# Token norms on all partitions, a table for the reciprocal root, and the order around four norm boundaries

## Chip, core and metric

One NeuronCore of a Trainium2 chip (trn2) runs the whole program. TensorE (PE) multiplies matrices, VectorE (DVE) and ScalarE (ACT) work elementwise, GpSimd (POOL) does little here, and SyncE (SP) issues most of the DMAs. The metric is the device time of one execution in microseconds (us), lower is better.

## The reference

A two-layer decoder trunk for one sequence of 256 tokens, D = 2048. Each layer has a token mixer (gated linear attention, GLA, in layer 0; forgetting attention, FoX, in layer 1) and a gated MLP with a short convolution (FFN). Each of the four sub-layers starts with the same norm, and a fifth stands at the end:

```
def rmsnorm(x, gain):
    xf = xf * lax.rsqrt(jnp.mean(xf * xf, axis=-1, keepdims=True) + NORM_EPS)
    return xf * gain

for i in range(2):
    mod = silu(c) @ w_mod[i] + b_mod[i]          # six vectors: shift, scale, gate, twice
    h = rmsnorm(x, norm_mix[i]) * (1.0 + sc_m) + sh_m
    x = x + (1.0 + g_m) * mixer(h)               # GLA, then FoX
    h = rmsnorm(x, norm_ffn[i]) * (1.0 + sc_f) + sh_f
    x = x + (1.0 + g_f) * conv_ffn(h, ...)
return rmsnorm(x, norm_final)
```

## The kernel before

**Layout.** The residual x stays in SBUF as `xT`: features on the 128 partitions, 16 slices m of 128 features, each 128x256 (256 tokens). A token's norm is therefore a sum over partitions and over slices.

**Products.** Every large product streams its weights from HBM in tiles k of 128x1024 float32 (SP issues the loads, five slots). A tile is split in two halves of a shorter format: ACT casts the high part (`wh`, L114), DVE subtracts (`wl`, L115). The activations are split in the same way (`h` high by ACT, L465; `h` low by DVE, L466 and L467), and PE adds three matmuls for each block: high times high (L544), low h times high w (L545), high h times low w (L546). `wh` and `wl` have four buffers each (AHEAD + 1), so the cast of tile k has to wait until PE is done with tile k-4. The last three tiles (TAIL) of a product that ends a sub-layer are held back and finished bank by bank, and DVE adds each bank to `xT` (L600).

**The norm.** While the tail runs, ACT squares the new slices two at a time (`sq`, L398, 128x512), DVE adds the early ones into `ss` (L404), and PE sums `ss` and the last two `sq` over partitions by matmuls against a vector of ones (L411: two columns of `pm`, tokens on partitions). `token_rstd` (L420 to L433) makes the reciprocal root of two columns on DVE: a bit shift as a first guess and three Newton steps, 15 small instructions. `bcast_cols` turns the two columns back into a row on all partitions: two diagonal matrices on DVE (`dg`, L367) and two matmuls (L369). `make_h` then makes the operand slice by slice: `hn` = xT times that row (L464), high part with scale and shift (L465), low part (L466, L467).

**Order.** A list scheduler sets the order of each engine's instructions when the kernel is built; `tc.issue_after` pins single instructions behind others. Engines run their queues strictly in that order. `gate` pins the casts of the four tiles that follow slice m=1 behind the last square and behind the low part of m=1.

**Side work.** The six modulation vectors of the next sub-layer are made beside the main work: weights by DMA, products and sums on DVE into `acc` (L250, L252, 128x1024), then `finish` reduces `acc` over partitions by PE transposes (L265) and ACT activations with an accumulated sum (L274). Ahead of FoX and of the second FFN two such finishes are deferred into the wait at the norm.

**The boundaries.** The prediction calls them A (start, into GLA), B (GLA into the first FFN), C (first FFN into FoX), D (FoX into the second FFN) and E (end: final norm, eight blocks of the output scaled by DVE and ACT, L1228 to L1233, and eight output DMAs, all on SP, L1234). FoX starts with a narrow product (L591 to L593) and has wide matmuls of 512 columns (L577 to L579).

## Time and profile before

| | |
|---|---|
| time, median of 3 runs | 2486.22 us (2484.94 to 2488.49) |
| the profiled execution | 2486.61 us, its span 2484.9 us |
| PE busy | 2421.4 us, 97% of the span |
| DVE busy | 1906.7 us, 77% |
| ACT busy | 1279.8 us, 52% |
| mean granted TensorE clock | 0.984 |

The span runs from the first instruction to the last on the profiler's clock; 1.7 us of the profiled execution lie around it. Times within the span are counted from its start. The granted clock is 1.00 at 2.4 GHz and 0.50 at 1.2 GHz.

### The profile page before, as it was taken

To read this page: it belongs to the slowest core of one execution; us is meant where nothing else is said; L and a number is where in the kernel's file an instruction comes from. 1 tells how busy PE (TensorE), PEld (TensorE's weight loads), DVE (VectorE), ACT (ScalarE), POOL (GpSimd) and SP (SyncE) were. 2 spreads that over 40 slices of the span, in tenths; PEclk is the share of its full clock that TensorE was granted. 3 is DMA by queue.
4 is the path that set the end of the run, shared out by engine and by line. 5 is a ranking of instruction groups with operands and counts; after the bars stand their busy time and mean duration, and the time that the engine had idled before them with its cause. 6 is when DMAs were issued, how large, how long until landed. Compare 5 with 4: busy or idle time off the path is not lost.

```text
span 2484.9 us, 47584 instructions
## 1 busy us (share of the span) xinstructions
PE 2421.4 (97%) x19242; PEld 2331.1 (94%) x19242; DVE 1906.7 (77%) x2570; ACT 1279.8 (52%) x1956; POOL 14.6 (1%) x35
## 2 busy tenths in 40 slices
PE   6999999899999999999999999999999999999998
PEld 6988899899999999999988888999999999999998
DVE  6776989886789999977587888887776777767544
ACT  2446554444655666543454555554655556565433
POOL 0000000000000000000000000000000000000000
PEclk7999999999999999999999999999999999999999
DMA  8897878798668998899589887687677777766553
GB/s 349 268 309 239 295 262 287 269 317 306 207 195 270 309 308 301 285 314 316 179 278 308 304 280 235 212 293 268 197 236 232 231 235 232 233 193 218 192 192 122
DMA packets 184314, 638.36 MB, mean 257 GB/s; under 512 B 23962, under 2 KB 24972, under 8 KB 183709
## 3 DMA queue, kind: packets, MB, share of 16 engines
q1 hardware_dynamic: 183704, 635.17, 77.1%
q8 instruction: 150, 2.46, 0.4%
q14 instruction: 72, 0.58, 0.1%
q10 hardware_dynamic: 388, 0.15, 0.0%
HBM read 633.14 MB, written 2.10 MB: 256 GB/s over the span
## 4 chain that ended last, share of the span: by engine, by line
PE 74%; DMA 11%; DVE 9%; issue 3%; ACT 2%; SPq 0%; DVEq 0%; ACTq 0%
PE pa L545 19%; PE pa L546 19%; PE pa L544 19%; DMA wm<-in_w_mod_dram 6%; PE pa L579 4%; PE pa L578 4%; PE pa L577 4%; DVE wl L115 4%; DVE acc L252 2%; DMA w<-in_ffn_w_down_dram 2%; DMA w<-in_ffn_w_up_dram 2%; ACT wh L114 1%; DMA w<-in_gla_w_out_dram 1%; PE pm L265 1%; PE pm L411 0%
## 5 line engine op out<-in xcount | busy, mean ns | idle before, releaser
L114 ACT CAST wh<-w 128x1024 fp32r<-128x1024 f32 x819 | 856.4, 1048 | 1033.7 <-PE pa L545 463.7
L115 DVE TENSOR_TENSOR wl<-w,wh 128x1024 fp32r<-128x1024 f32 x819 | 994.8, 1218 | 365.0 <-ACT wh L114 354.2
L544 PE MATMUL pa<-h,wh 128*128 128x256 f32 x3584 | 990.1, 278 | 10.1 <-ACT h L465 5.6
L545 PE MATMUL pa<-h,wh 128*128 128x256 f32 x3584 | 993.1, 278 | 1.1 <-DVE h L467 0.9
L546 PE MATMUL pa<-h,wl 128*128 128x256 f32 x3584 | 991.7, 278 | 1.5 <-DVE wl L115 1.5
L544 PEld LDWEIGHTS pa<-h,wh 128*128 128x128 f32 x3584 | 674.2, 189 | 12.0 <-ACT h L465 6.6
L546 PEld LDWEIGHTS pa<-h,wl 128*128 128x128 f32 x3584 | 675.0, 189 | 4.4 <-issue 2.3
L545 PEld LDWEIGHTS pa<-h,wh 128*128 128x128 f32 x3584 | 676.9, 189 | 2.0 <-DVE h L467 1.7
L252 DVE SCALAR_TENSOR_TENSOR acc<-wm,cT,acc 128x1024 f32<-128x1024 f32 x352 | 450.7, 1280 | 125.2 <-DMA wm<-in_w_mod_dram 123.5
L544 PE MATMUL pa<-op,wh 128*128 128x256 f32 x1920 | 527.2, 277 | 5.2 <-DVE xT L600 2.9
L545 PE MATMUL pa<-op,wh 128*128 128x256 f32 x1920 | 526.8, 277 | 2.0 <-DVE op L483 2.0
L546 PE MATMUL pa<-op,wl 128*128 128x256 f32 x1920 | 518.4, 278 | 1.6 <-DVE wl L115 1.0
L544 PEld LDWEIGHTS pa<-op,wh 128*128 128x128 f32 x1920 | 360.8, 188 | 6.6 <-DVE xT L600 3.4
L545 PEld LDWEIGHTS pa<-op,wh 128*128 128x128 f32 x1920 | 361.3, 188 | 2.2 <-DVE op L483 2.2
L546 PEld LDWEIGHTS pa<-op,wl 128*128 128x128 f32 x1920 | 354.9, 188 | 4.3 <-DVE wl L115 4.0
L578 PE MATMUL pa<-wh,h 128*128 128x512 f32 x512 | 200.4, 392 | 0.0
L577 PE MATMUL pa<-wh,h 128*128 128x512 f32 x512 | 199.2, 392 | 0.6 <-ACT wh L114 0.6
L579 PE MATMUL pa<-wl,h 128*128 128x512 f32 x512 | 193.9, 395 | 0.6 <-DVE wl L115 0.5
L577 PEld LDWEIGHTS pa<-wh,h 128*128 128x128 f32 x512 | 96.4, 188 | 20.7 <-ACT wh L114 1.0
L579 PEld LDWEIGHTS pa<-wl,h 128*128 128x128 f32 x512 | 95.9, 188 | 20.8 <-DVE wl L115 2.0
L578 PEld LDWEIGHTS pa<-wh,h 128*128 128x128 f32 x512 | 96.2, 188 | 19.8 <-issue 0.2
L1043 ACT ACTIVATE y<-u,cw 128x256 f32<-128x256 f32 x176 | 101.8, 600 | 17.1 <-DVE act L1059 14.7
(236 smaller groups left out, 1392.7 us busy)
## 6 DMA issues: line engine op xcount, KB each, us to landing
wm<-in_w_mod_dram SPq DMA_DIRECT2D x352, 512.0 KB, 5.2
w<-in_ffn_w_up_dram SPq DMA_DIRECT2D x320, 512.0 KB, 4.5
w<-in_ffn_w_down_dram SPq DMA_DIRECT2D x176, 512.0 KB, 4.6
w<-in_fox_w_in_dram SPq DMA_DIRECT2D x128, 512.0 KB, 5.2
...
```

What stands on the lines that cost most here:

```text
L114: nc.scalar.copy(out=hi, in_=src)
L115: order["v"] = nc.vector.tensor_tensor(out=lo, in0=src, in1=hi.bitcast(F32), op=ALU.subtract).ins
L252: nc.vector.scalar_tensor_tensor(out=st["a"], in0=wt[:, j, :], scalar=col, in1=st["a"], op0=ALU.mult, op1=ALU.add)
L265: nc.tensor.transpose(pt[:, m * P:(m + 1) * P], st["a"][:, (q0 + m) * P:(q0 + m + 1) * P], ident)
L544: nc.tensor.matmul(o, wh[:, ms], rh, start=(first and m % 2 == 0), stop=False, skip_group_check=True)
L545: nc.tensor.matmul(o, wh[:, ms], rl, start=False, stop=False, skip_group_check=True)
L546: nc.tensor.matmul(o, wl[:, ms], rh, start=False, stop=last, skip_group_check=True)
L577: nc.tensor.matmul(o, lh[:, ts_], wh[:, hs_], start=first, stop=False)
L578: nc.tensor.matmul(o, ll[:, ts_], wh[:, hs_], start=False, stop=False)
L579: nc.tensor.matmul(o, lh[:, ts_], wl[:, hs_], start=False, stop=last)
L1043: nc.scalar.activation(y, u, AF.Identity, scale=cw[:, l * 3 + 2, r:r + 1], bias=cw[:, 6 + l, r:r + 1])
```

## The change

Six things change.

1. The sum over partitions uses a held matrix `onesD` (all entries 1/D) as one operand, so that the mean lands on all partitions at once as 128x256. `half_sum` first adds the two halves of `ss` on DVE, and the last square is split in two of 128x256. The final norm (`fin`) keeps two columns.
2. `token_rstd` takes a table function of ACT (`Abs_reciprocal_sqrt`) and one third-order step of five DVE instructions, on 128x256 (on 128x2 at E). The broadcast (`dg`, L369, the copy of `rb`) goes. A small activation `warm` behind the square of m=12 brings the table load forward.
3. Deferred finishes (C and D) reduce by eight matmuls against a column of ones instead of transposes and ACT sums; one of the two runs ahead of the tail.
4. `split_to` is called ahead of the tail, and the gate now holds three casts instead of four, behind the high part (`hot`) and the low part of m=1. The `hn` of m=1 to 3 are pinned behind the low part of the slice ahead.
5. The helper for other reciprocal roots (GLA and FoX, off the boundaries) loses two DVE instructions per call.
6. At E four of the eight output DMAs are issued by ACT.

```diff
-        for j in range(2):
-            for tt in range(TT):
-                order["s"] = nc.tensor.matmul(ss["p"][:, tt:tt + 1], sq[:, j, tt * P:(tt + 1) * P], one, ...)
+        if not fin:
+            order["s"] = nc.tensor.matmul(ss["p"][:, :T], onesD, sq, start=first, stop=last, skip_group_check=True).ins
+            return
...
+        if end and m == KT - 2:
+            for j in range(2):
+                order["a"] = nc.scalar.activation(sq[:, j, :], xT[:, m + j, :], AF.Square).ins
+                token_sum(sq[:, j, :], False, j == 1)
+            return
...
             if m == KT - NTS:
-                token_sum(ss["t"], True, False)
-            token_sum(sq, False, m == KT - 2)
+                warm = tmp.tile([P, 1], F32, tag="warm", bufs=1, name=nm("warm"))
+                nc.scalar.activation(warm, sq[:, 0, 0:1], AF.Abs_reciprocal_sqrt, bias=epsc)
+                half_sum()
+                token_sum(ss["t"][:, 0, :], True, False)
+            for j in range(2):
+                token_sum(sq[:, j, :], False, False)
...
+    def token_rstd(q, n_):
+        nc.scalar.activation(q, ss["p"][:, :n_], AF.Abs_reciprocal_sqrt, bias=epsc)
+        ...
+        nc.vector.scalar_tensor_tensor(out=t, in0=ss["p"][:, :n_], scalar=EPS, in1=q, op0=ALU.add, op1=ALU.mult)
+        nc.vector.tensor_tensor(out=t, in0=t, in1=q, op=ALU.mult)
+        nc.vector.tensor_scalar(out=p, in0=t, scalar1=0.375, scalar2=-1.25, op0=ALU.mult, op1=ALU.add)
+        nc.vector.tensor_tensor(out=t, in0=t, in1=p, op=ALU.mult)
+        nc.vector.scalar_tensor_tensor(out=q, in0=t, scalar=1.875, in1=q, op0=ALU.add, op1=ALU.mult)
...
-        pb = bcast_cols([rs[:, 0:1], rs[:, 1:2]], -1.0)
-            if m == 2:
-                nc.scalar.copy(out=rb, in_=pb[:, :T])
-            nc.vector.tensor_tensor(out=t, in0=xT[:, m, :], in1=pb[:, :T] if m < 2 else rb, op=ALU.mult)
-            nc.scalar.activation(hi, t, AF.Identity, scale=sc, bias=sh)
+            with ExitStack() as es:
+                if 0 < m < 4:
+                    es.enter_context(tc.issue_after(st["lo"]))
+                nc.vector.tensor_tensor(out=t, in0=xT[:, m, :], in1=rb, op=ALU.mult)
+            hot = nc.scalar.activation(hi, t, AF.Identity, scale=sc, bias=sh).ins
             ...
             ins = nc.vector.tensor_tensor(out=lo, in0=t, in1=hi.bitcast(F32), op=ALU.subtract).ins
+            st["lo"] = ins
             if m == 1:
-                gate["n"], gate["ins"] = AHEAD + 1, [order["a"], ins]
+                gate["n"], gate["ins"] = AHEAD, [hot, ins]
...
         if done is not None:
+            split_to(min(fetched["use"] + 1, len(plan)))
+            if deferred:
+                deferred.pop(0)()
...
+                if defer:
+                    pt = psA.tile([P, 512], F32, tag="a", name=nm("pt"))
+                    for m in range(mn):
+                        nc.tensor.matmul(pt[:, m:m + 1], st["a"][:, m * P:(m + 1) * P], one, start=(m == 0), ...)
...
-            nc.sync.dma_start(out=out[0, tt * P:(tt + 1) * P, cs], in_=dst)
+            (nc.sync if tt == 0 else nc.scalar).dma_start(out=out[0, tt * P:(tt + 1) * P, cs], in_=dst)
```

What this does to the queues is seen at two boundaries. DVE at B, from the low part of slice 1 on; `hn` and `h` are the slices of the operand (m counted from 0), `wl` the low halves of the weight tiles k=1 to 4 of the first FFN. Before:

```order
L467 TENSOR_TENSOR h_5040<-hn_5046,h_5040 128x256
L115 TENSOR_TENSOR wl_5060<-w_4831,wh_5059 128x1024
L115 TENSOR_TENSOR wl_5066<-w_4861,wh_5065 128x1024
L115 TENSOR_TENSOR wl_5072<-w_4891,wh_5071 128x1024
L466 TENSOR_SCALAR hn_5052<-hn_5052,mod 128x256
L464 TENSOR_TENSOR hn_5191<-xT,rb_5029 128x256
L466 TENSOR_SCALAR hn_5103<-hn_5103,mod 128x256
L466 TENSOR_SCALAR hn_5147<-hn_5147,mod 128x256
L467 TENSOR_TENSOR h_5040<-hn_5052,h_5040 128x256
L115 TENSOR_TENSOR wl_5111<-w_5057,wh_5110 128x1024
L467 TENSOR_TENSOR h_5040<-hn_5103,h_5040 128x256
```

The last row is the low part of slice 3; the row above it is tile k=4. And now, DVE at B from the low part of slice 2 on (first row) to that of slice 3 (last row); `wl_5114` is tile k=5, `wl_5158` tile k=6:

```order
L487 TENSOR_TENSOR h_5000<-hn_5011,h_5000 128x256
L484 TENSOR_TENSOR hn_5062<-xT,rb_4981 128x256
L484 TENSOR_TENSOR hn_5106<-xT,rb_4981 128x256
L484 TENSOR_TENSOR hn_5150<-xT,rb_4981 128x256
L115 TENSOR_TENSOR wl_5114<-w_5022,wh_5113 128x1024
L199 COPY cw<-pm_5144 128x352
L254 TENSOR_SCALAR acc_5097<-wm_5058,cT 128x1024
...
L486 TENSOR_SCALAR hn_5062<-hn_5062,mod 128x256
...
L256 SCALAR_TENSOR_TENSOR acc_5097<-wm_5060,cT,acc_5097 128x1024
L115 TENSOR_TENSOR wl_5158<-w_5028,wh_5157 128x1024
L487 TENSOR_TENSOR h_5000<-hn_5062,h_5000 128x256
```

The low part of slice 3 moved from behind tile k=4 to behind tile k=6 and two side sums (the rows left out are one L484 and two L486).

ACT at B, from the square of m=12 to the casts of the next tiles (`wh`). Before:

```order
L398 ACTIVATE sq_4963<-xT 128x512
L274 ACTIVATE pm_4791,red_4781<-pm_4791 128x128 x2
L398 ACTIVATE sq_4994<-xT 128x512
L114 CAST wh_5059<-w_4831 128x1024
L114 CAST wh_5065<-w_4861 128x1024
L114 CAST wh_5071<-w_4891 128x1024
L465 ACTIVATE h_5040<-hn_5041,mod 128x256
L465 ACTIVATE h_5040<-hn_5046,mod 128x256
```

And now:

```order
L419 ACTIVATE sq_4943<-xT 128x512
L285 ACTIVATE pm_4771,red_4761<-pm_4771 128x128
L423 ACT_TABLE_LOAD
L423 ACTIVATE warm_4945<-sq_4943,epsc 128x1
L416 ACTIVATE sq_4972<-xT 128x256
...
L448 ACTIVATE rb_4981<-pm_4948,epsc 128x256
L485 ACTIVATE h_5000<-hn_5001,mod 128x256
L485 ACTIVATE h_5000<-hn_5006,mod 128x256
L114 CAST wh_5018<-w_4811 128x1024
L114 CAST wh_5024<-w_4841 128x1024
L114 CAST wh_5030<-w_4871 128x1024
```

The three casts moved from ahead of `h` to behind its slice 1, and a table load came in ahead of the last square. At C and D the casts and the load move in the same way.

PE at C, from the sum over partitions to the first matmuls of FoX. Before:

```order
L411 MATMUL pm_14251<-ones,ss_12874 128x1 x4
L411 MATMUL pm_14251<-ones,sq_14249 128x1 x4
L411 MATMUL pm_14251<-ones,sq_14280 128x1 x4
L265 MATMUL pt_14305<-ident,acc_12177 128x128 x4
...
L369 MATMUL pm_14345<-dg_14346,ones 128x128
L369 MATMUL pm_14345<-dg_14349,ones 128x128
L591 MATMUL pm_14353<-h_14354,wh_14179 128x256
L577 MATMUL pa_14518<-wh_14373,h_14354 128x512
```

And now:

```order
L439 MATMUL pm_14224<-ss_12833,onesD 128x256
L439 MATMUL pm_14224<-sq_14219,onesD 128x256 x2
L439 MATMUL pm_14224<-sq_14248,onesD 128x256 x2
L268 MATMUL pt_14262<-ones,acc_12980 128x1 x8
L618 MATMUL pm_14272<-h_14273,wh_14138 128x256
L619 MATMUL pm_14272<-h_14273,wh_14138 128x256
L620 MATMUL pm_14272<-h_14273,wl_14139 128x256
L618 MATMUL pm_14272<-h_14273,wh_14138 128x256
L604 MATMUL pa_14436<-wh_14291,h_14273 128x512
```

Sixteen transposes (L265, three more rows of four are left out) and the broadcast left the wait; eight matmuls of one column came in.

## Rows read from the trace of the kernel before

**Rows 1.** The page, busy time of each engine over the span (share, instructions).

```profile
PE 2421.4 (97%) x19242; PEld 2331.1 (94%) x19242; DVE 1906.7 (77%) x2570; ACT 1279.8 (52%) x1956; POOL 14.6 (1%) x35
```

**Rows 2.** Timeline of PE at B: start, duration, engine, line and operation, idle time before it and what ended that.

```profile
486.31 0.79 PE L369 MATMUL pm<-dg,ones 128*128 128x128 f32 x2 [2.81 <-DVE dg L367]
...
489.33 1.22 PE L544 MATMUL pa<-h,wh 128*128 128x256 f32 x4 [1.15 <-ACT h L465]
```

**Rows 3.** Timeline of DVE at B: first step of the reciprocal root, first slice of the operand, low part of slice 2, tile k=4, low part of slice 3.

```profile
483.54 0.16 DVE L420 TENSOR_SCALAR tv<-pm 128x2 f32<-128x2 f32 x1 [1.91 <-PE pm L411]
...
488.23 0.75 DVE L464 TENSOR_TENSOR hn<-xT,pm 128x256 f32<-128x256 f32 x2 [1.77 <-PE pm L369]
...
496.49 0.41 DVE L467 TENSOR_TENSOR h<-hn,h 128x256 fp32r<-128x256 f32 x1
496.82 1.21 DVE L115 TENSOR_TENSOR wl<-w,wh 128x1024 fp32r<-128x1024 f32 x1
497.96 0.41 DVE L467 TENSOR_TENSOR h<-hn,h 128x256 fp32r<-128x256 f32 x1
```

**Rows 4.** Timeline of ACT at B: the last sum of side work, the last square, the three casts, the copy of the row, and the casts of tiles k=4 and k=5, which wait for PE.

```profile
481.06 0.26 ACT L274 ACTIVATE pm<-pm 128x128 f32<-128x128 f32 x1
481.24 0.19 ACT L274 ACTIVATION_READ_ACCUMULATOR pm<-pm 128x1 f32 x1
481.33 0.62 ACT L398 ACTIVATE sq<-xT 128x512 f32<-128x512 f32 x1
481.85 2.92 ACT L114 CAST wh<-w 128x1024 fp32r<-128x1024 f32 x3
...
489.68 0.35 ACT L460 COPY rb<-pm 128x256 f32<-128x256 f32 x1
...
494.37 1.05 ACT L114 CAST wh<-w 128x1024 fp32r<-128x1024 f32 x1 [1.90 <-PE pa L545]
...
497.18 1.05 ACT L114 CAST wh<-w 128x1024 fp32r<-128x1024 f32 x1 [0.62 <-PE pa L545]
```

**Rows 5.** Durations by line and form over the whole span: count, then busy time in us and mean ns of one, then idle time before.

```profile
L115 DVE TENSOR_TENSOR wl<-w,wh 128x1024 fp32r<-128x1024 f32 x816 | 993.5, 1221 | 364.0 <-ACT wh L114 353.2 <-DMA w<-in_ffn_w_up_dram 3.9 <-PE pa L579 1.6
L252 DVE SCALAR_TENSOR_TENSOR acc<-wm,cT,acc 128x1024 f32<-128x1024 f32 x352 | 450.7, 1280 | 125.2 <-DMA wm<-in_w_mod_dram 123.5
L600 DVE SCALAR_TENSOR_TENSOR xT<-pa,mod,xT 128x256 f32<-128x256 f32 x64 | 27.2, 476 | 11.4 <-PE pa L546 11.4
L466 DVE TENSOR_SCALAR hn<-hn,mod 128x256 f32<-128x256 f32 x64 | 24.6, 406 | 2.1 <-ACT h L465 2.0
```

**Rows 6.** Timeline of ACT inside FoX: a table load and the activation behind it.

```profile
1284.51 1.28 ACT L620 ACT_TABLE_LOAD   x1
1285.81 0.42 ACT L620 ACTIVATE lfe<-lfe 16x256 f32<-16x256 f32 x1
```

**Rows 7.** Stretches at B: start and end, length, busy time (count) of PE, PEld, DVE, ACT and POOL, granted clock, DMA share, GB/s.

```profile
482.00:484.00 2.00, 1.50 (x11) 1.41 (x11) 0.39 (x3) 2.00 (x3) 0.00 (x0) 0.70 0.02 8
...
493.00:494.00 1.00, 1.00 (x10) 1.00 (x10) 1.00 (x1) 0.00 (x0) 0.00 (x0) 0.98 0.93 377
```

**Rows 8.** Timeline of PE at C.

```profile
1231.73 2.04 PE L411 MATMUL pm<-ones,sq 128*128 128x1 f32 x16
1233.63 3.58 PE L265 MATMUL pt<-ident,acc 128*128 128x128 f32 x16
...
1239.42 0.39 PE L591 MATMUL pm<-h,wh 128*128 128x256 f32 x1 [1.74 <-ACT h L465]
1239.65 1.10 PE L577 MATMUL pa<-wh,h 128*128 128x512 f32 x4
```

**Rows 9.** Stretches at C, columns as in rows 7.

```profile
1234.00:1236.00 2.00, 2.00 (x12) 2.00 (x11) 1.93 (x12) 2.00 (x7) 0.00 (x0) 0.50 0.00 0
1236.00:1238.00 2.00, 1.68 (x10) 1.49 (x8) 1.01 (x6) 2.00 (x16) 0.00 (x0) 0.71 0.00 0
...
1242.00:1244.00 2.00, 1.24 (x7) 0.92 (x7) 2.00 (x3) 1.41 (x3) 0.00 (x0) 1.00 0.00 0
```

**Rows 10.** Timeline of DVE and of ACT at D and C: first slice of the operand (DVE, D), its high part (ACT, D), then the last square and the first high part at C (ACT).

```profile
1742.53 0.75 DVE L464 TENSOR_TENSOR hn<-xT,pm 128x256 f32<-128x256 f32 x2 [1.13 <-PE pm L369]
...
1744.53 0.59 ACT L465 ACTIVATE h<-hn,mod 128x256 fp32r<-128x256 f32 x1
...
1232.03 0.63 ACT L398 ACTIVATE sq<-xT 128x512 f32<-128x512 f32 x1 [1.16 <-DVE xT L600]
...
1238.79 0.58 ACT L465 ACTIVATE h<-hn,mod 128x256 fp32r<-128x256 f32 x1
```

**Rows 11.** Timeline at E, all engines: the reciprocal root's first and last step, the scaling on ACT, the output DMAs' issue on SP's queue.

```profile
2473.56 0.16 DVE L420 TENSOR_SCALAR tv<-pm 128x2 f32<-128x2 f32 x1 [0.36 <-PE pm L411]
...
2476.12 1.95 ACT L1233 ACTIVATE ot<-ot,tq 128x512 f32<-128x512 f32 x3 [3.94 <-DVE tq L433]
2476.51 4.47 SPq L1234 DMA_DIRECT2D out_dram<-ot  x8
```

**Rows 12.** Timeline of ACT at the start: a DMA issued on ACT's queue.

```profile
0.81 0.42 ACTq L150 DMA_DIRECT2D rows<-in_norm_mix_dram  x1
```

**Rows 13.** Timeline at A: DVE's wait for the sum over partitions, PE's wait for the first low half of a weight tile.

```profile
42.13 0.16 DVE L420 TENSOR_SCALAR tv<-pm 128x2 f32<-128x2 f32 x1 [1.47 <-PE pm L411]
...
64.71 0.58 PE L546 MATMUL pa<-h,wl 128*128 128x256 f32 x1 [1.23 <-DVE wl L115]
```

More of the change, by code (lines that the diff above doesn't have):

```diff
@@ L260, in finish @@
                 m0, mn = c0 // P, width // P
[L261 to L263 removed]
+                if defer:
+                    pt = psA.tile([P, 512], F32, tag="a", name=nm("pt"))
+                    for m in range(mn):
+                        nc.tensor.matmul(pt[:, m:m + 1], st["a"][:, m * P:(m + 1) * P], one, start=(m == 0),
+                                         stop=(m == mn - 1), skip_group_check=True)
+                    red = pt
+                else:
+                    red = tmp.tile([P, 8], F32, tag="red", name=nm("red"))
+                for q0 in range(0, 0 if defer else mn, 4):
+                    pt = psA.tile([P, 512], F32, tag="a", name=nm("pt")) if wide else misc()
                     for m in range(min(4, mn - q0)):
@@ new lines, in token_sum @@
+        if not fin:
+            order["s"] = nc.tensor.matmul(ss["p"][:, :T], onesD, sq, start=first, stop=last, skip_group_check=True).ins
+            return
+        for tt in range(TT):
+            order["s"] = nc.tensor.matmul(ss["p"][:, tt:tt + 1], sq[:, tt * P:(tt + 1) * P], onesD[:, 0:1],
+                                          start=(first and tt == 0), stop=(last and tt == 1),
+                                          skip_group_check=True).ins
+    def token_rstd(q, n_):
+        nc.scalar.activation(q, ss["p"][:, :n_], AF.Abs_reciprocal_sqrt, bias=epsc)
+        t = tmp.tile([P, T], F32, tag="ra", bufs=1, name=nm("ra"))[:, :n_]
+        p = tmp.tile([P, T + 48], F32, tag="rp", bufs=1, name=nm("rp"))[:, :n_]
+        nc.vector.scalar_tensor_tensor(out=t, in0=ss["p"][:, :n_], scalar=EPS, in1=q, op0=ALU.add, op1=ALU.mult)
[3 more added lines that the diff above has]
+        nc.vector.scalar_tensor_tensor(out=q, in0=t, scalar=1.875, in1=q, op0=ALU.add, op1=ALU.mult)
@@ L504, in next_w, with split_to @@
             run, look = min(run, STAGE - i), 1
-        while fetched["split"] < min(i + 1 + run, len(plan)):
+        split_to(min(i + 1 + run, len(plan)), look)
+        return splits.popleft()
+    def split_to(end, look=RING - 1):
+        while fetched["split"] < end:
             while fetched["load"] < min(fetched["split"] + look, len(plan)):
```

57 lines of the change are left out of this document (20 added, 37 removed).

## The prediction

> **What bounds the kernel now.** I read the page's busy times first: PE is busy 97% of the span [rows 1], so 63.5 us in all are left to it as waits and only those, or a change of its clock, can be won or lost. The timeline then says where they lie: at the start (A), at the three boundaries in between (B, C, D) and at the end (E). At B the GLA product is followed by the sums of the norm, and the next product starts at 489.33 [rows 2]. The reader should see who is late in turn: DVE waits 1.91 us for the sums over partitions and starts the reciprocal root at 483.54; PE waits 2.81 us for DVE's diagonal matrices; DVE waits 1.77 us for the broadcast and makes the first slice at 488.23 [rows 2, 3]; PE then waits for its high part. Behind the boundary the order matters: ACT's cast of tile k=4 waits for PE at 494.37 [rows 4], since a fifth tile has to have the buffer of the first, and the low parts of slices 2 and 3 are done at 496.9 and 498.4 with one weight tile between them [rows 3].
>
> The clock is the other thing to read. At B it falls to half in the wait (0.70 in 482 to 484) and is back at 493 [rows 7], 3.7 us after the product began. At C it falls too, but comes back in 1236 to 1238 [rows 9], while PE runs the sixteen transposes of the side work [rows 8], so FoX begins at full clock.
>
> **The change part by part.**
>
> *The sums.* Twelve matmuls of one column (24 records) become five of 256 columns. Behind the last square one matmul is left. No row has its shape; from the transposes, 3.58 / 16 = 0.22 a record [rows 8], and two records for it, I take 0.4, against half of the 2.04 us of the sixteen L411 records [rows 8]: 0.6 won, with 0 and 0.8 as ends. Against that stands the table load ahead of the last square: 1.30 from its start to the next activation [rows 6], and about 0.2 for `warm`. At C ACT sat idle for 1.16 us there [rows 10], so some 0.4 show, and the second half square adds 0.2: the sums come at the same time as before. I take the same for D and E. At B nothing covers it, since side sums sit right ahead of the square [rows 4]: 1.5, and another side sum of 0.45 between the half squares, so the squares end 2.0 us later; 0.4 + 0.1 behind them instead of 483.54 - 481.95 = 1.6 [rows 3, 4] leaves the sums 0.9 late.
>
> The Trainium skill, page "ScalarE: Activation LUTs", section "What ACT_TABLE_LOAD costs", has another price: 1283 ns for the load and a drain of some 1380 ns, 2.66 us for a switch. The row shows the load and 0.02 us behind it, no drain. By the page B, C and D would each lose 1.4 us more, E some, and the time would be about 2492.
>
> *The root.* Now 4.69 us pass at B from the first step to the first slice [rows 3], 0.6 of it for other matmuls between the two halves of the broadcast. After: ACT on 128x256 out of PSUM 0.35 (the copy in rows 4) to 0.5, 0.1 to DVE, one DVE step out of PSUM 0.48 and four of 0.41 [rows 5], each with some 0.04 of waiting for the one before: 0.45 + 0.1 + 0.52 + 1.8 = 2.9 us. So 1.8 are won at B, 1.8 - 0.6 = 1.2 elsewhere, less 0.17 at C and D, where a small step of the side work now stands among the five.
>
> *The side sums at C and D.* Their ACT train kept the high part waiting: at D the first slice was there at 1742.53 + 0.42 and `h` came at 1744.53 [rows 10]. This goes.
>
> *The early split* does nothing by itself: the three casts in the wait at B are followed by that of k=4 [rows 4], so they are tiles 1 to 3, and tile 0 was split before the wait already. What the gate does is a loss: those casts ran in the wait and now stand behind slice 1's high part.
>
> *A.* DVE is late here. Its wait of 1.47 us [rows 13] goes, and three slices move behind the modulation, so the latter is ready about 2.2 us earlier. But the first tile's cast now stands behind slice 1: `h` 0.6, two DVE steps, `h` again 0.6, cast 1.05, `wl` 1.2 [rows 4, 5, 10] put the first low-half matmul near 63.7 against 64.71 [rows 13]. I take +0.7 (0 to 1.3).
>
> *B.* Sums 0.9 later, root 1.8 shorter: the product begins 0.6 to 0.9 earlier, and 0.4 more comes from matmuls that stood in tile 0. Then comes the queue. The order shows the low part of slice 3 behind tile k=6 instead of k=4. Tile 6 needs the buffer of tile 2, so its cast starts when PE has finished k=2; PE needs that low part four matmuls into k=3. At the least PE waits for cast 1.05 + `wl` 1.22 + low part 0.35, less 0.45 of matmuls that it can do first: 2.2 us. DVE makes it longer. From the low part of slice 2 to that of slice 3 its queue holds four `hn` of 0.34, tiles 5 and 6 (2.3), a copy (0.4), two side sums (0.7 and 1.2), three scalings (1.0) and the low part (0.35), 7.3 us by the pitches behind rows 3 and 5. With the root done at 487.6, three casts and three tiles of `wl` behind it and tile 4 after those, I get the low part of slice 2 at 496.9 and that of slice 3 at about 504.8. PE could use it at 499.8, and before it passed that point at 500.3 (done with k=1 at 497.1 [rows 4], 2.75 for k=2 and 0.45). So PE idles some 5 us and comes out 4.5 behind. Idling that long may cost clock: at B now it is 3.7 us at half speed [rows 2, 7], 1.8 lost; I take 0.5. B: -5.0 (-6.3 to +0.9).
>
> *C.* From the sums' end (1233.77) to `h` 5.0 us pass [rows 8, 10]; after, 2.9 + 0.17 + 0.42 = 3.5, so PE begins 1.5 earlier, but only the narrow matmuls. The first wide one needs a cast that now stands behind slice 1: 0.6 + 1.15 + 0.6 + 1.05 = 3.4 after `h` starts, at 1240.5, against 1239.65 [rows 8]. 0.85 is lost; some 1.0 us of idling inside the first tile (PE has 1.24 busy of 2.00 in 1242 to 1244 [rows 9]) is won back. And without the transposes the clock should still be low: if for as long as at B now, 1.8 lost, some of it under later waits; I take 0.45. C: -0.3 (-1.7 to +1.6).
>
> The Trainium skill, page "TensorE: Matmul & The Clock Gate", section "Part 4: PE-mode transpose", says that transposes don't lift the clock. Rows 8 and 9 show the clock rising while they run. By the page C would lose nothing when they go, and the sum would be better by 0.45.
>
> *D.* Root 1.0 and the train 1.5 [rows 10] make +2.5. The clock is as before. The low parts of slices 2 and 3 stand behind tiles 4 and 5 there, which gives back 0.9 (0 to 2). +1.6 (0.5 to 2.5).
>
> *E.* The root on two columns takes 2.5 us now [rows 11]; after, 0.35 + five steps of 0.2 + one DVE instruction of 0.42 between them: 1.75. Sums: +0.25. SP needs 4.47 us to issue eight DMAs [rows 11], 0.56 each; ACT will scale for 1.95 us and then issue four of 0.42 [rows 12] to 0.56, done 4.0 after the root, against 4.9 now. +1.8 (0.5 to 2.5).
>
> *The rest*: two DVE steps fewer in each call of the other helper, tables loaded inside the FFNs, one finish ahead of the tail: PE has work there, nothing changes.
>
> **Sum:** 0.7 - 5.0 - 0.3 + 1.6 + 1.8 = -1.2, a loss of 1.2 us. Of the profiled execution's 2486.61 (its span and 1.7 around it) that makes 2487.8; it lies 0.39 above the median of the runs, so I give 2487.4. About 0.2%, 5 us, is what can be told from no change here.
>
> **The rivals.**
>
> *Slower: the pause at B pulls the clock down.* An idle PE of 5 us in the middle of a product is about as long as B's wait; if the granted clock falls there and comes back as late as in rows 7, B loses 1.8 instead of 0.5, and if C loses its full 1.8 too, and D's low parts take the whole 2, the sum is -1.2 - 1.3 - 1.4 - 1.1 = -5.0: 2491.2. It decides when the clock in B's third and fourth tile is 0.50. For it: rows 7, 9. Against: DVE is the later one there, so a slower PE is partly hidden.
>
> *Faster: no pause at B.* If DVE reaches the low part of slice 3 in time (side sums early, casts early), B is +0.9 and the sum 4.7: 2481.5; with C at +1.6 and D at 2.5, 2478.7. It decides when DVE does the low part of slice 3 before PE is through tile 2. Against it: the order, with a buffer that forbids it.
>
> *The table costs more than rows 6 say.* The new function has no row here. If it takes 1.5 us instead of 0.45, or a load in front of the squares holds ACT 1 us longer, each of the four boundaries from B to E loses 1.05: 2491.6. It decides in ACT's rows between the square of m=12 and the root. For it speaks only that no row shows the function; against it, all of ACT's rows of 256 columns lie between 0.35 and 0.60 [rows 4, 10]. The drain of the skill's page, 1.4 us at B, C and D, would be this rival's mechanism.
>
> **How the numbers follow.** The forecast, B paused and the rest small: 0.55. Slower by the clock 0.15, by tables or the root 0.1. Faster, no pause or a much cheaper end: 0.2. The forecast's own range is 2483 to 2491; to hold 8 in 10 it reaches into both sides: 2480 to 2493. Faster by over 0.2%: 0.2; within: 0.55; slower: 0.25.
>
> **What would show it.** In the profile after: at B an idle of 4 to 5 us of PE ahead of a low-part matmul (high w), released by DVE's low part, some 11 us after the product starts; the root in 2.9 us from ACT's table function to the first `hn`; at C the clock at 0.50 when the wide matmuls start, near 1240.5; at D PE starting 2.5 us earlier; at E the span's tail 1.8 us shorter. The forecast is wrong if B shows no such idle, or if a row of the new table function or of a load on the path is far from 0.45 and 1.3 us.

## The result: 0.3% slower

| | before | after |
|---|---|---|
| time, median of 19 runs each | 2487.15 us (2481.67 to 2491.03) | 2494.2 us (2489.03 to 2500.01) |
| ratio to before | | 1.0032, 95% interval 1.0025 to 1.0040 |
| the profiled execution | 2486.61 us | 2492.91 us, its span 2491.2 |

The ratio means 8.0 us more (6.2 to 9.9). The prediction's 2487.4 and its whole range, 2480 to 2493, lie below the time after.

**Where the time went.** First the page's busy times after; they answer to [rows 1].

```profile
PE 2418.2 (97%) x19206; PEld 2325.2 (93%) x19206; DVE 1903.2 (76%) x2506; ACT 1283.1 (52%) x1908; POOL 16.6 (1%) x35
```

PE was busy 3.2 us less in a span that is 6.3 us longer: its waits grew. Next, PE at B, from the first matmul of the FFN (answers to [rows 2]). L568 to L570 are the three product matmuls, L484 to L487 make a slice of the operand: L484 `hn`, L485 its high part, L486 and L487 its low part.

```profile
487.94 1.22 PE L568 MATMUL pa<-h,wh 128*128 128x256 f32 x4 [2.27 <-ACT h L485]
...
496.70 0.39 PE L569 MATMUL pa<-h,wh 128*128 128x256 f32 x1 [0.99 <-DVE h L487]
...
503.90 0.39 PE L569 MATMUL pa<-h,wh 128*128 128x256 f32 x1 [4.19 <-DVE h L487]
```

The product waits twice for a low part: 0.99 us for slice 2 and 4.19 us for slice 3. DVE's timeline over the same stretch (answers to [rows 3]; L451 to L455 are the root's steps) shows why.

```profile
484.66 0.42 DVE L451 SCALAR_TENSOR_TENSOR ra<-pm,rb 128x256 f32<-128x256 f32 x1 [1.58 <-ACT rb L448]
...
486.83 0.42 DVE L484 TENSOR_TENSOR hn<-xT,rb 128x256 f32<-128x256 f32 x1
...
494.65 1.22 DVE L115 TENSOR_TENSOR wl<-w,wh 128x1024 fp32r<-128x1024 f32 x1
...
496.22 0.42 DVE L487 TENSOR_TENSOR h<-hn,h 128x256 fp32r<-128x256 f32 x1
496.56 1.09 DVE L484 TENSOR_TENSOR hn<-xT,rb 128x256 f32<-128x256 f32 x3
497.56 1.23 DVE L115 TENSOR_TENSOR wl<-w,wh 128x1024 fp32r<-128x1024 f32 x1
...
501.09 1.29 DVE L256 SCALAR_TENSOR_TENSOR acc<-wm,cT,acc 128x1024 f32<-128x1024 f32 x1
502.28 1.23 DVE L115 TENSOR_TENSOR wl<-w,wh 128x1024 fp32r<-128x1024 f32 x1
503.42 0.77 DVE L487 TENSOR_TENSOR h<-hn,h 128x256 fp32r<-128x256 f32 x2
```

DVE has no wait in these rows behind the first. The low part of slice 2 is at 496.22, that of slice 3 at 503.42, with two weight tiles (k=5 and k=6) and two side sums between them. Now ACT at B (answers to [rows 4]): the load for `warm` (L423), the table function (L448), the high part, the casts.

```profile
480.70 1.28 ACT L423 ACT_TABLE_LOAD   x1
482.00 0.29 ACT L423 ACTIVATE warm<-sq,epsc 128x1 f32<-128x1 f32 x1
...
484.16 0.47 ACT L448 ACTIVATE rb<-pm,epsc 128x256 f32<-128x256 f32 x1 [0.97 <-PE pm L439]
487.29 0.60 ACT L485 ACTIVATE h<-hn,mod 128x256 fp32r<-128x256 f32 x1 [2.66 <-DVE hn L484]
489.17 0.60 ACT L485 ACTIVATE h<-hn,mod 128x256 fp32r<-128x256 f32 x1 [1.28 <-DVE hn L484]
489.67 2.93 ACT L114 CAST wh<-w 128x1024 fp32r<-128x1024 f32 x3
...
499.23 1.05 ACT L114 CAST wh<-w 128x1024 fp32r<-128x1024 f32 x1 [0.62 <-ACT h L485]
```

The root takes 2.67 us (484.16 to 486.83), and the load is followed by the next activation after 0.02 us. The last row is the cast of tile k=6, which starts 0.13 us after PE is done with tile k=2 (its next tile begins at 499.10) and is over at 500.28; DVE comes to the `wl` of that tile at 502.28, behind the side sums. So about half of the second pause is the buffer and half is DVE's queue. The granted clock, columns as in [rows 7, 9], at B and at C:

```profile
502.00:504.00 2.00, 0.10 (x1) 0.10 (x1) 2.00 (x4) 0.00 (x0) 0.00 (x0) 1.00 0.96 305
504.00:506.00 2.00, 2.00 (x13) 2.00 (x14) 2.00 (x7) 0.60 (x1) 0.00 (x0) 0.72 0.86 330
506.00:508.00 2.00, 2.00 (x12) 2.00 (x11) 1.60 (x5) 0.36 (x1) 0.00 (x0) 0.50 0.44 166
508.00:510.00 2.00, 2.00 (x18) 2.00 (x18) 1.28 (x2) 0.69 (x1) 0.00 (x0) 0.93 0.04 8
...
1246.00:1248.00 2.00, 1.47 (x4) 0.88 (x4) 1.32 (x4) 1.99 (x3) 0.00 (x0) 0.50 0.00 0
1248.00:1250.00 2.00, 2.00 (x6) 1.52 (x6) 2.00 (x2) 1.94 (x3) 0.00 (x0) 0.50 0.08 8
```

In this execution PE idles at full clock in the pause; the clock falls when the pause is over and PE works again, and is back soon after 508. PE at C (answers to [rows 8]): the tail's matmuls, the finish that now runs ahead of them (L268), the narrow product (L618), the first wide matmul (L604).

```profile
1227.78 0.28 PE L570 MATMUL pa<-op,wl 128*128 128x256 f32 x1
1227.90 1.84 PE L268 MATMUL pt<-ones,acc 128*128 128x1 f32 x16
1229.60 0.36 PE L568 MATMUL pa<-op,wh 128*128 128x256 f32 x1
...
1244.79 0.38 PE L618 MATMUL pm<-h,wh 128*128 128x256 f32 x1 [2.14 <-ACT h L485]
...
1247.60 0.80 PE L604 MATMUL pa<-wh,h 128*128 128x512 f32 x1 [0.36 <-ACT wh L114]
```

The finish is sixteen records of one column. PE's stream of product matmuls stands still for them from 1227.90 to 1229.60: 1.70 us. At D the same finish stands from 1735.17 to 1736.87, again 1.70. The wide matmuls start 2.81 us after the narrow ones; before it was 0.23 [rows 8]. Last, E (answers to [rows 11]):

```profile
2480.58 0.26 ACT L448 ACTIVATE tq<-pm,epsc 128x2 f32<-128x2 f32 x1 [0.84 <-PE pm L442]
...
2482.62 1.34 ACT L1260 ACTIVATE ot<-ot,tq 128x512 f32<-128x512 f32 x2 [1.78 <-DVE tq L455]
...
2483.38 0.37 ACTq L1261 DMA_DIRECT2D out_dram<-ot  x1
...
2483.99 2.81 ACTq L1261 DMA_DIRECT2D out_dram<-ot  x3
```

The first row is the table function; the scaling starts 2.04 us behind its start, where the old root took 2.5 [rows 11]. Half of the output DMAs are now issued by ACT.

**A ledger by boundary.** From PE's rows four stretches were measured in every kernel: B from the end of the last GLA matmul to the end of the 192nd matmul (eight tiles) of the first FFN; C and D likewise (96 wide matmuls at C); E from the end of the last product matmul to the end of the span. Column F is the finish ahead of the tail, 2 x 1.70, which lies ahead of C and D. "Rows" is the sum of the five against the kernel before, "runs" the difference by the measured ratio, with its interval; each ratio is to runs of the kernel before on the same chip. All in us. The kernels are told below.

| kernel | B | C | D | E | F | rows | runs |
|---|---|---|---|---|---|---|---|
| before | 33.91 | 35.78 | 34.41 | 14.25 | 0 | | |
| after | 39.75 | 37.30 | 32.40 | 12.98 | 3.4 | +7.5 | +8.0 (6.2 to 9.9) |
| pin_off | 33.68 | 36.61 | 31.33 | 12.75 | 3.4 | -0.6 | -2.7 (-5.5 to 0.0) |
| pop_in_wait | 39.41 | 37.26 | 32.26 | 12.61 | 0 | +3.2 | +5.2 (3.0 to 7.7) |
| gate_back | 42.87 | 37.08 | 34.09 | 12.66 | 3.4 | +11.8 | +13.7 (10.4 to 16.9) |
| cast_behind_root | 33.31 | 34.23 | 32.25 | 12.66 | 0 | -5.9 | -4.7 (-7.0 to -2.5) |
| pin_on_before | 41.44 | 37.74 | 35.08 | 14.25 | 0 | +10.2 | +14.2 (9.9 to 18.2) |
| no_warm | 32.36 | 34.07 | 30.69 | 13.29 | 0 | -7.9 | -8.0 (-10.7 to -5.2) |
| out_on_sp | 33.15 | 35.39 | 32.62 | 12.61 | 0 | -4.6 | -7.7 (-10.2 to -5.2) |
| pop_ahead | 33.13 | 34.69 | 31.33 | 12.66 | 3.4 | -3.1 | -2.7 (-5.0 to -0.2) |
| pin_two | 35.59 | 36.37 | 34.87 | 12.90 | 3.4 | +4.8 | +5.7 (2.7 to 8.9) |
| transposes_in_wait | 33.79 | 37.27 | 33.27 | 12.64 | 0 | -1.4 | -2.0 (-5.7 to 1.7) |
| no_warm_out_sp | 32.73 | 33.98 | 30.46 | 13.27 | 0 | -7.9 | -6.7 (-9.7 to -4.0) |

For eleven of the twelve the rows fall into the interval of the runs; for out_on_sp they fall 0.6 short of it. One profile's stretch isn't exact either: cast_behind_root and out_on_sp have the same order on every engine up to E, and their C differs by 1.16 us, D by 0.37. The first FFN behind its eight tiles takes 711.70 to 724.16 us without order, and single runs differ by as much, so one profile's span is a worse measure than these stretches. (The second FFN behind its eight tiles is the same in all, 700.43 to 700.48.) A is not in the table: whether GLA's product begins at 63.1, as in after, or at 60.5 to 61.4, its output product ends between 479.3 and 481.5 in the first group and between 478.2 and 481.8 in the second.

### The profile page after: what moved, and what is told of

Same layout as the page of the kernel before. It is cut to its first block, busy times and chain, and to the rows that moved or that the text cites. A ratio compares the mean times of both kernels' runs of the same rounds, so it can differ in the third digit from the quotient of the medians.

```text
span 2491.2 us, 47398 instructions
## 1 busy us (share of the span) xinstructions
PE 2418.2 (97%) x19206; PEld 2325.2 (93%) x19206; DVE 1903.2 (76%) x2506; ACT 1283.1 (52%) x1908; POOL 16.6 (1%) x35
## 4 chain that ended last, share of the span: by engine, by line
PE 78%; DMA 10%; DVE 8%; issue 2%; ACT 2%; DVEq 0%; SPq 0%; ACTq 0%
PE pa L569 20%; PE pa L570 20%; PE pa L568 20%; DMA wm<-in_w_mod_dram 6%; PE pa L604 4%; PE pa L605 4%; PE pa L606 4%; DVE wl L115 3%; DVE acc L256 2%; DMA w<-in_gla_w_out_dram 2%; DMA w<-in_ffn_w_down_dram 1%; ACT wh L114 1%; PE pm L276 1%; DVE op L504 0%; DMA w<-in_gla_w_in_dram 0%
## 5 line engine op out<-in xcount | busy, mean ns | idle before, releaser
L568 PE MATMUL pa<-h,wh 128*128 128x256 f32 x3584 | 988.9, 278 | 12.1 <-ACT h L485 4.9
L570 PE MATMUL pa<-h,wl 128*128 128x256 f32 x3584 | 991.7, 278 | 0.9 <-DVE wl L115 0.8
L568 PEld LDWEIGHTS pa<-h,wh 128*128 128x128 f32 x3584 | 673.2, 189 | 13.9 <-ACT h L485 5.3
L570 PEld LDWEIGHTS pa<-h,wl 128*128 128x128 f32 x3584 | 675.4, 189 | 3.9 <-issue 2.3
L256 DVE SCALAR_TENSOR_TENSOR acc<-wm,cT,acc 128x1024 f32<-128x1024 f32 x352 | 451.8, 1283 | 116.8 <-DMA wm<-in_w_mod_dram 114.6
L568 PE MATMUL pa<-op,wh 128*128 128x256 f32 x1920 | 526.6, 277 | 6.9 <-DVE xT L627 4.5
L570 PE MATMUL pa<-op,wl 128*128 128x256 f32 x1920 | 517.3, 278 | 3.0 <-DVE wl L115 2.2
L568 PEld LDWEIGHTS pa<-op,wh 128*128 128x128 f32 x1920 | 360.6, 188 | 8.3 <-DVE xT L627 4.7
L570 PEld LDWEIGHTS pa<-op,wl 128*128 128x128 f32 x1920 | 354.0, 188 | 6.8 <-DVE wl L115 6.8
L604 PE MATMUL pa<-wh,h 128*128 128x512 f32 x512 | 200.7, 395 | 1.1 <-ACT wh L114 1.1
L604 PEld LDWEIGHTS pa<-wh,h 128*128 128x128 f32 x512 | 96.7, 189 | 21.5 <-ACT wh L114 1.8
```

The lines of the kernel that those rows point to most:

```text
L256: nc.vector.scalar_tensor_tensor(out=st["a"], in0=wt[:, j, :], scalar=col, in1=st["a"], op0=ALU.mult, op1=ALU.add)
L568: nc.tensor.matmul(o, wh[:, ms], rh, start=(first and m % 2 == 0), stop=False, skip_group_check=True)
L570: nc.tensor.matmul(o, wl[:, ms], rh, start=False, stop=last, skip_group_check=True)
L604: nc.tensor.matmul(o, lh[:, ts_], wh[:, hs_], start=first, stop=False)
```

## The experiments

Line numbers move a little between the kernels.

**The pin alone (theory: the pause at B is the loss).** pin_off is the changed kernel with `hn` of slices 1 to 3 free:

```diff
-            with ExitStack() as es:
-                if 0 < m < 4:
-                    es.enter_context(tc.issue_after(st["lo"]))
-                nc.vector.tensor_tensor(out=t, in0=xT[:, m, :], in1=rb, op=ALU.mult)
+            nc.vector.tensor_tensor(out=t, in0=xT[:, m, :], in1=rb, op=ALU.mult)
```

> The changed kernel without the pin that puts the hn of slices 1 to 3 behind the low part of the slice ahead; all else as changed. The order then has the low part of slice 3 at B behind weight tile 4 again, not 6. Theory (the pin makes PE's pause of 4.2 us and most of the 1.0 us at B): both pauses at B under 0.5 us, about 4.5 us less in all, 2489 to 2490. Rival 1 (the new norm itself costs the time): the pause may go, the time stays near 2494. Rival 2 (the weight and modulation loads set the pace of the first FFN): the pause at B goes, but the wait between the halves of the down product at 1111 to 1116 grows by as much, 2493 to 2495.

Measured: 2482.03 us, 0.9989 (0.9978 to 1.0000). DVE's timeline at B; here L484 is the low part:

```profile
497.09 0.42 DVE L484 TENSOR_TENSOR h<-hn,h 128x256 fp32r<-128x256 f32 x1
497.42 1.22 DVE L115 TENSOR_TENSOR wl<-w,wh 128x1024 fp32r<-128x1024 f32 x1
...
498.99 1.08 DVE L484 TENSOR_TENSOR h<-hn,h 128x256 fp32r<-128x256 f32 x3
```

One tile stands between the low parts of slices 2 and 3, as in [rows 3], and PE no longer idles: B is 6.1 us shorter than after, more than the 5.2 of the two pauses, and the clock, once it is back from the wait, stays at 1.00 there. The gain was larger than expected: 8.1 us by the rows, 10.7 by the ratios, against 4.5.

The opposite edit, pin_on_before, puts the same pin into the kernel before:

```diff
-            nc.vector.tensor_tensor(out=t, in0=xT[:, m, :], in1=pb[:, :T] if m < 2 else rb, op=ALU.mult)
+            with ExitStack() as es:
+                if 0 < m < 4:
+                    es.enter_context(tc.issue_after(st["lo"]))
+                nc.vector.tensor_tensor(out=t, in0=xT[:, m, :], in1=pb[:, :T] if m < 2 else rb, op=ALU.mult)
...
+            st["lo"] = ins
```

> The kernel before with one thing added: the hn of slices 1 to 3 pinned behind the low part of the slice ahead. The old norm, gate and finishes stay. The order then has the low part of slice 3 at B behind weight tile 6 and two side sums, as in the changed kernel. Theory (the pin alone makes the pause): PE idles some 4 to 5 us ahead of tile 3's low-part matmuls at B, the first eight tiles take some 30.5 us instead of 24.0, and the kernel is 5 to 8 us slower than before. Rival (the pause needs the new norm or the late casts, since before the casts run in the wait): under 2 us, no difference to be told.

Measured: 2498.54 us, 1.0057 (1.0040 to 1.0073). PE's timeline at B has the same pause with none of the rest of the change:

```profile
503.76 0.58 PE L549 MATMUL pa<-h,wh 128*128 128x256 f32 x1 [4.49 <-DVE h L470]
```

So the pin makes the pause by itself. It cost more than expected (5 to 8): 10.2 us by the rows, 11.6 by the medians. Here the clock fell inside the pause and stayed at 0.50 for 6.8 us, twice as long as in after:

```profile
502.00:504.00 2.00, 0.24 (x1) 0.24 (x2) 2.00 (x5) 0.00 (x0) 0.00 (x0) 0.53 0.98 330
```

pin_two keeps the pin on slices 1 and 2 and frees slice 3:

```diff
-                if 0 < m < 4:
+                if 0 < m < 3:
```

> The changed kernel with the pin on hn of m=1 and 2 only; that of m=3 is free. The low part of slice 3 then stands behind tile k=4, right behind that of slice 2, instead of behind tile k=6. If the pause is made by that one pin alone, the pause ahead of the low part of slice 3 (4.19 us in the changed kernel) is gone, that ahead of slice 2 (0.99) stays near 1 to 1.5, the first eight tiles at B take 25 to 27 us instead of 30.67, and the time is 4 to 8 us below the changed kernel: a ratio of 0.9990 to 1.0015. Rival: the pins of slices 1 and 2 delay DVE as well, and the first eight tiles stay at 28 us or more.

Measured: 2491.14 us, 1.0023 (1.0011 to 1.0036), so the time was not what I expected. PE's timeline at B and at D:

```profile
499.94 0.38 PE L569 MATMUL pa<-h,wh 128*128 128x256 f32 x1 [1.79 <-DVE h L487]
...
1763.64 0.39 PE L569 MATMUL pa<-h,wh 128*128 128x256 f32 x1 [1.91 <-DVE h L487]
```

At B it went by the theory: no second pause, one of 1.79 us, B 4.2 us shorter than after. But the scheduler moved the low parts at D as well, a new pause of 1.91 us came there, and D grew by 2.5. What is left is inside the noise of the ratio.

**The finish ahead of the tail.** pop_in_wait drops two lines of the changed kernel:

```diff
-            if deferred:
-                deferred.pop(0)()
```

> The changed kernel with both deferred finishes in the wait at the norm, none ahead of the tail. Theory: sixteen records of one column held PE for 1.7 us in the dense stream ahead of the tail at C and at D, and cost nothing in the wait, where PE idles 2 us: 3.4 us less, near 2490.8. Rival: in the wait they stand ahead of the first matmul and delay the modulation column that slice 0 needs, so that 1 to 2 us come back at each place: no change, 2493 to 2495.

Measured: 2490.86 us, 1.0021 (1.0012 to 1.0031). That is 2.7 us won by the ratios. The waits at C and D stay what they were with both finishes in them (6.72 and 6.71 us from the last product matmul to the first, after 6.74 and 6.74), so in the wait the second finish is free.

pop_ahead adds the two lines to the reordered kernel that follows below:

> The kernel cast_behind_root with one finish of two ahead of the tail again, as in the changed kernel. Theory: eight matmuls of one column cost PE 1.7 us in the dense stream at C and at D (the last matmul of the product comes 1.7 later at each) and shorten neither wait (6.8): 3.4 us more than cast_behind_root. Rival (they fill PE gaps of the tail): no change.

Measured: 2483.1 us, 0.9989 (0.9980 to 0.9999), against 0.9981 without: 2.0 us by the ratios. Both differences agree with 3.4, but neither would show a loss by itself: each is uncertain by some 3 us to either side. The rows are sharper. FoX's output product, at whose tail the finish of D stands, takes 89.15 to 89.16 us in the five kernels with the finish ahead of the tail and 87.32 to 87.39 in the eight without it, before among them: 1.8 us. The product that ends at C differs by several us between any two kernels, so there the stop of 1.70 us in PE's stream is all that shows.

**The gate.** gate_back gives the changed kernel the old gate, four casts behind the last square:

```diff
-                gate["n"], gate["ins"] = AHEAD, [hot, ins]
+                gate["n"], gate["ins"] = AHEAD + 1, [order["a"], ins]
```

> The changed kernel with the old gate: four casts, behind the last square and the low part of slice 1. The order then has three casts (2.9 us) ahead of the table function of the root on ACT. Theory: root late by 1.9 us at B, C and D (it waits 1.0 for the sums now, the casts take 2.9), C's wide matmuls start with slice 0 again (2.6 won), A's first cast is early (1.7 won), the pause at B stays: +1 us, 2494 to 2497. Rival (the gate is the main loss): 2488 to 2490.

Measured: 2498.65 us, 1.0055 (1.0042 to 1.0068), worse than expected. ACT's timeline at B:

```profile
485.06 2.92 ACT L114 CAST wh<-w 128x1024 fp32r<-128x1024 f32 x3
487.89 0.46 ACT L448 ACTIVATE rb<-pm,epsc 128x256 f32<-128x256 f32 x1
```

The root is now ACT's, and it stands behind three casts; all three waits grow by 1.8 us (B 8.69 to 10.44, C and D 6.74 to 8.54), and the second pause at B grows to 5.34. At C the wide matmuls do come 0.38 behind the narrow ones, as the theory had it. The old gate, free while the root was DVE's, doesn't fit the new root.

cast_behind_root is the reordered kernel: no pin, both finishes in the wait, and the casts pinned behind the table function itself, before the high parts (`wl` stays behind the low part of slice 1):

```diff
-                gate["n"], gate["ins"] = AHEAD, [hot, ins]
+                gate["n"], gate["ins"] = AHEAD, [order["r"], ins]
...
+        with ExitStack() as es:
+            if pins[0] is not None:
+                es.enter_context(tc.issue_after(pins[0]))
+            nc.scalar.copy(out=hi, in_=src)
+        with ExitStack() as es:
+            if pins[1] is not None:
+                es.enter_context(tc.issue_after(pins[1]))
+            order["v"] = nc.vector.tensor_tensor(out=lo, in0=src, in1=hi.bitcast(F32), op=ALU.subtract).ins
```

> The changed kernel without the pin, with both finishes in the wait, and with the three casts pinned behind the table function of the root instead of behind slice 1, their low halves behind the low part of slice 1. ACT idles 2.66 us there at B. Theory: sum of the parts, 4.5 (pause at B) + 3.4 (records ahead of the tail) + 2.6 (casts at C) + up to 1 at A = 11 us less than the changed kernel, 2483, which is 4 us faster than before. Rival (new norm no faster than the old one): no better than before, 2487 or above.

Measured: 2480.6 us, 0.9981 (0.9972 to 0.9990), as expected. ACT casts while DVE does the root's five steps, and PE at C finds a cast tile as soon as it has its operand:

```profile
1238.67 0.39 PE L618 MATMUL pm<-h,wh 128*128 128x256 f32 x1 [0.43 <-ACT h L488]
1238.89 1.66 PE L604 MATMUL pa<-wh,h 128*128 128x512 f32 x4
```

0.22 us lie between narrow and wide, where after had 2.81.

**The clock at C.** transposes_in_wait is cast_behind_root with the finishes at C and D by transposes and ACT sums, as before:

```diff
-                if defer:
-                    pt = psA.tile([P, 512], F32, tag="a", name=nm("pt"))
-                    for m in range(mn):
-                        nc.tensor.matmul(pt[:, m:m + 1], st["a"][:, m * P:(m + 1) * P], one, ...)
-                    red = pt
```

> The reordered kernel of the earlier run (casts behind the root, no pin, finishes in the wait), but deferred finishes at C and D reduce by transposes and ACT sums again. The clock theory of the prediction: with the transposes back the granted clock is 1.00 when the first wide matmuls of FoX run, where it is 0.50 for some 4 us without them, and the first eight tiles there get shorter by up to 1.8 us. Rival: DVE sets the pace there, so the clock costs nothing, and those tiles stay at 27.3 us (within 0.3). Both expect the ACT sums to hold up the high part again: the waits at C and D grow by 0.5 to 1.5 us each, and the time is 1 to 3 us above the reordered kernel.

Measured: 2484.68 us, 0.9992 (0.9977 to 1.0007), 2.7 us above cast_behind_root by the ratios. PE's timeline at C, and the stretches behind it:

```profile
1239.50 1.91 PE L275 MATMUL pt<-ident,acc 128*128 128x128 f32 x16
1244.67 0.58 PE L611 MATMUL pm<-h,wh 128*128 128x256 f32 x1 [3.27 <-ACT h L481]
```

```profile
1240.00:1242.00 2.00, 1.41 (x13) 1.17 (x11) 1.66 (x5) 2.00 (x4) 0.00 (x0) 1.00 0.00 0
...
1244.00:1246.00 2.00, 1.32 (x4) 1.09 (x5) 1.31 (x4) 2.00 (x11) 0.00 (x0) 0.50 0.00 0
```

The transposes run at full clock, and the clock falls all the same behind the wait. So the first theory falls. The rival doesn't hold as it stands: the tiles took 28.99 us, not 27.3, with ACT busy with the sums (16 activations and their reads) and the clock at 0.50 for their first 5.6 us. A cleaner comparison is before against cast_behind_root, with these stretches of the latter:

```profile
1238.00:1240.00 2.00, 1.57 (x8) 1.19 (x7) 2.00 (x8) 2.00 (x5) 0.00 (x0) 0.79 0.00 0
1240.00:1242.00 2.00, 2.00 (x8) 1.74 (x7) 2.00 (x4) 0.09 (x1) 0.00 (x0) 0.50 0.00 0
1242.00:1244.00 2.00, 2.00 (x11) 1.69 (x10) 2.00 (x3) 1.05 (x1) 0.00 (x0) 0.86 0.42 106
```

Before has the clock back by then [rows 9], cast_behind_root at 0.50 for 3.4 us, and the first eight tiles take 27.22 us in both. DVE is busy 2.00 of 2.00 there, so 3.4 us of a slower PE fit under it. A longer stretch doesn't fit. In out_on_sp, which has the same order up to E, the clock is at 0.50 for the first 5.5 us of the tiles, and they take 28.22, 1.0 more, with DVE as busy (one pair of executions):

```profile
1240.00:1242.00 2.00, 2.00 (x8) 1.71 (x7) 2.00 (x3) 0.00 (x0) 0.00 (x0) 0.50 0.07 10
1242.00:1244.00 2.00, 2.00 (x9) 1.66 (x8) 2.00 (x5) 1.47 (x2) 0.00 (x0) 0.57 0.88 233
```

How long the clock stays low at a boundary, 3.4 or 6.8 us, differs between these two executions of one order. The waits at C and D grew by 1.1 us each with the ACT sums back, as both theories had it.

**Two small parts.** no_warm is cast_behind_root without the two lines of `warm`:

```diff
-                warm = tmp.tile([P, 1], F32, tag="warm", bufs=1, name=nm("warm"))
-                nc.scalar.activation(warm, sq[:, 0, 0:1], AF.Abs_reciprocal_sqrt, bias=epsc)
```

> The kernel cast_behind_root without the small warm activation: the table load then stands between the last square and the root, where ACT idles about 0.9 us for the sums. Theory: the load does not wait for the sums and hides behind them; at B the wait from the last matmul to the first is 0.9 us shorter (7.9 instead of 8.8), at C and D 0.35 shorter (6.4 instead of 6.8), at the end the same: 2 us less than cast_behind_root, 0.997 of before. Rival (the load starts only with the root's own wait): the root is 1.3 us behind the sums, B unchanged, C, D and the end 0.4 longer: 1 us more than cast_behind_root.

Measured: 2478.29 us, 0.9968 (0.9957 to 0.9979). ACT's timeline at C in no_warm:

```profile
1237.43 0.81 ACT L422 ACTIVATE sq<-xT 128x256 f32<-128x256 f32 x2 [0.76 <-DVE xT L625]
1238.26 1.28 ACT L452 ACT_TABLE_LOAD   x1
1239.55 0.47 ACT L452 ACTIVATE rb<-pm,epsc 128x256 f32<-128x256 f32 x1
```

The load now runs behind the last square, while PE sums it. The waits at B, C and D get 0.36, 0.26 and 0.26 us shorter than in cast_behind_root; at E, where less stands between square and root, 0.6 is lost. That makes 0.25 us in all, where the rows have 2.0 and the ratios 3.2 with intervals that overlap. Most of the 2.0 lies in D's first eight tiles (24.16 us, 25.46 in cast_behind_root), where the clock was at 0.50 for 3.4 us instead of 6.7; that the missing `warm` did this is not shown.

out_on_sp is cast_behind_root with all eight output DMAs on SP again:

```diff
-            (nc.sync if tt == 0 else nc.scalar).dma_start(out=out[0, tt * P:(tt + 1) * P, cs], in_=dst)
+            nc.sync.dma_start(out=out[0, tt * P:(tt + 1) * P, cs], in_=dst)
```

> The kernel cast_behind_root with all eight output DMAs on SP again. Theory: SP issues eight at 0.56 each behind the root, 4.5 us, while with two queues ACT's four (0.94 each in the trace of the changed kernel) end 4.2 after the root: the stretch from the last product matmul to the end grows by 0.3 to 1.2 us from 12.7, nothing else changes. Rival (landing decides, not issue): no change.

Measured: 2479.82 us, 0.9969 (0.9959 to 0.9979). E takes 12.61 us with the issue on SP alone, 12.66 with half of it on ACT. The ratio is lower by 0.0012, with intervals that overlap; no row shows a gain. In out_on_sp:

```profile
2472.27 4.48 SPq L1261 DMA_DIRECT2D out_dram<-ot  x8
```

4.48 / 8 = 0.56 us an issue on SP; the three behind one another on ACT took 2.81 / 3 = 0.94 each in after. The split buys nothing.

no_warm_out_sp has both edits.

> The reordered kernel of the earlier run without the warm activation and with all eight output DMAs on SP: both edits left the time the same or a little better by themselves (0.9968 and 0.9969 against the kernel before). From their stages: B, C and D shorter by 0.3 each, the end the same within 0.2. 0.9960 to 0.9975 against the kernel before if the two are independent. Rival: what was won by either was chance between runs, and the ratio is that of the reordered kernel, 0.998.

Measured: 2479.74 us, 0.9973 (0.9961 to 0.9984). The intervals of the three ratios overlap, and the rival's 0.998 lies in this one too, so the run doesn't tell whether the two gains add. By the rows it is 2.0 us better than cast_behind_root, and the clock at D was again low for 3.4 us. E is 13.27 here, so `warm` should stay at E. A kernel with `warm` at E alone was not run.

**The early split**, without a run: built without the call of `split_to` ahead of the tail, the changed kernel has the same instructions in the same order on PE, DVE and ACT.

No run takes the helper (change 5) or the sums and the root by themselves. FoX between its first wide tiles and its output product takes 379.72 to 381.76 us, before 381.50 and after 380.82, so nothing of the helper shows there.

## Why the prediction was wrong

By its own terms, as gains in us:

| term | predicted | measured |
|---|---|---|
| A | +0.7 | -0.25 at the first low-half matmul; not in the sum |
| B | -5.0 | -5.8 |
| C | -0.3 | -1.5 |
| D | +1.6 | +2.0 |
| E | +1.8 | +1.3 |
| the rest, one finish ahead of the tail | 0 | -3.4 |
| sum | -1.2 | -7.5 |

*The step that failed* is "one finish ahead of the tail: PE has work there, nothing changes". PE's having work is what makes it cost: each record added to its dense stream is time, 1.70 us at C and at D. I took the finish for side work that hides, and didn't ask where it goes. The prediction's first paragraph has the same gap: it counts only PE's waits and its clock as what can be won or lost, and not work added to PE. In the wait the finish was free (pop_in_wait). The term is 3.4 of the 6.3 us by which the sum was off; C is 1.2 of the rest, B 0.8, A 0.7.

*B* was right in its mechanism and nearly in its size. The low part of slice 2 was forecast for 496.9 and done at 496.6, that of slice 3 for 504.8 and done near 503.9. The first pause, 0.99, was not foreseen; the second, 4.19, was called 5. What I had put too low is the clock: 0.5 was taken, but the clock is at 0.50 from about 504.9 to 508.3, 1.7 lost. Together, 0.99 + 4.19 + 1.7 = 6.9, that is what the eight tiles took more than before (31.06 against 24.20); 1.0 came back in the wait. The fall of the clock was the slower rival's mechanism, and at B it came about. The same rival's other part, a full loss of 1.8 by the clock at C, didn't.

*C* is the second term that was mis-sized. The wait got 1.6 shorter, as forecast (1.5), and the first wide matmul came 2.81 after the narrow one, so that it stands 0.99 later behind the product's end than before, where 0.85 was forecast (its own summands, 3.4 behind 1237.3, give 1.0). What failed is the 1.0 of idling that was to be won back inside the first tiles: after took 27.75 us for them, 0.5 more than before. The clock was at 0.50 for 4.8 us of them; how much of the 0.5 is the clock's is not separated. Between narrow and wide pin_off still has 2.16, cast_behind_root 0.22: some 2.0 are the gate's, which puts the casts behind slice 1's high part, and 0.6 the pin's, by which that high part waits for its `hn` (1.28 us at B above).

*A*: the first cast behind slice 1's high part put the first product matmul at 63.09 instead of 61.35. The first low-half matmul, which the forecast of 63.7 was for, came at 64.96, against 64.71 before [rows 13]: 0.25 lost where 0.7 was to be won.

*D and E*: right in sign. At D the wait got 2.67 shorter (2.5 forecast), and the first eight tiles gave back 0.7 (0.9 forecast for the low parts behind later tiles); the clock was low for longer there too, and the two aren't separated. E gained 1.3 of the 1.8. Its gain is that of the sums and the root; the split issue, which I had counted in, gives nothing.

*The root and the table*: 2.9 us were priced for the root and 2.67 came; the new function took 0.47 (0.45 priced). "Tables cost more" is out. The Trainium skill, page "ScalarE: Activation LUTs", section "What ACT_TABLE_LOAD costs", adds a drain of some 1380 ns to a load of 1283 ns; the load agrees with 1.28 in the rows, and no drain shows: `warm` starts 0.02 us behind the load.

*The early split* was called a step that does nothing, and it is one; the gate beside it is a loss, as the prediction said.

*Transposes and the clock*: the Trainium skill, page "TensorE: Matmul & The Clock Gate", section "Part 4: PE-mode transpose", says that they don't lift it. The rows of the kernel before speak against it: PE ran nothing but the sixteen transposes from 1233.63 [rows 8] to 1237.01, where the first broadcast matmul starts, the clock was at 0.50, and it was back near 1237.1 (0.71 in 1236 to 1238 [rows 9]). The run with the transposes adds nothing, as the clock had not fallen when they ran. The forecast's price of 0.45 for the clock at C is neither confirmed nor excluded.

The forecast's likeliest case was right about what happens at B; the time left its range through a step that was passed over in a line.
